# Forget gate of a hybrid decoder block: log-sums formed with heads on partitions instead of tokens

## The chip, the cores and the metric

One core of one Trainium2 chip runs the whole kernel as one program. The metric is device time in microseconds for one execution, median of several runs; lower is better. The core's engines run side by side, each in the order of its own queue: TensorE (PE, matrix products; its weight loads are shown as PEld), VectorE (DVE), ScalarE (ACT), GpSimd (POOL) and SyncE (SP), which here only issues DMA transfers. Products land in PSUM, a memory of eight banks of 128 partitions x 512 f32; everything else is in SBUF, 128 partitions.

## The reference, cut to what matters

One decoder layer on 256 tokens with 1024 channels: RMS norm, one wide input projection, two attention branches of 8 heads each (MoBA and FoX), a gated merge, an output projection and a gated feed-forward with a short convolution, all in float32. The change touches only the forget gate of the FoX branch:

```python
log_f = jax.nn.log_sigmoid(f_logit + b_forget)        # (tokens, 8 heads)
c = jnp.cumsum(log_f, axis=-1)                          # along the 256 tokens, per head
s = q.k * scale + c[t] - c[s]                           # FoX scores: query t, key s
s = where(s_pos <= t_pos, s, -1e30)
p = softmax(s)
```

`f_logit` is the normed input times an 8-column weight. So 8 x 256 numbers are made, summed along the tokens, and used twice: as `c[t]`, one number per query (with tokens on partitions), and as `c[s]`, a row of 256 numbers that every partition needs.

## The kernel before, in words

Tokens are two tiles of 128 (`NT = 2`), channels are eight tiles of 128 (`KT = 8`). Every weight product is made from split operands: a weight half of 128x1024 f32 comes by DMA into `raw`, ScalarE copies its rounded part into `whi` (L131), VectorE subtracts to get the rest, `wlo` (L132), and TensorE makes three products instead of one (L243, L253 for the input projection, L466 to L468 for gate and up projections, and so on). `load` keeps the splitting five halves ahead of use; there are six buffers each for `whi` and `wlo` (`HB = 6`, `AHEAD = 5`) and three for `raw`.

The order on TensorE is that of the program text (`manual_schedule`). All other engines are ordered by a planner that works by priorities, which follow the program text; what stands in `with soon():` gets a priority as if it stood 45 instructions earlier. Each engine then works strictly in the planned order, waiting where an operand is not there.

Around the forget gate the program text runs: `project(3, ...)` (FoX queries), transposes of the MoBA queries, `forget_a`, transposes of the MoBA keys, first half of `project(4)` (FoX keys), `forget_b`, MoBA scores and softmax of head pairs 0 and 1, second half of `project(4)`, `forget_c`, MoBA scores of pairs 2 and 3, `project(5)` (FoX values), `forget_d`, `forget_bias`, then `turn(0)` (transposes of the MoBA probabilities, L432), `gate(0)` and so on; the FoX scores, which read the bias, come after `gate(2)`. `gate(c)` makes 48 products from two weight halves into one bank, and VectorE takes it out into `gates[:, c]` (L475).

The forget gate's own steps:

- `forget_a` makes the logits with heads on partitions: eight products (L318), four at a time in four column groups of 32, so that four partial sums stand on partitions 0-7, 32-39, 64-71 and 96-103 of one bank. Beside them two products (L321) spread `rs`, the norm's factor per token, over all partitions (`rsB`). VectorE copies both out (L323, L324).
- `forget_b` adds up the four partial sums and transposes at once: per token tile, a product with the logits as stationary operand and `sel` (128x8, ones where partition mod 32 is the head) as moving one (L331). The result has tokens on partitions, `z[128, 2, 8]`. Factor and bias are put on by L334, and a chain of small instructions on [128, 16] between ScalarE and VectorE makes the log-sigmoid (L337 to L351).
- `forget_c` sums along the tokens by three products with a triangle of ones and a square of ones (L357 to L359); VectorE copies the result to `cc` (L360), the form with tokens on partitions.
- `forget_d` transposes `cc` back to heads on partitions (L365), copies it out (L367), writes it to a DRAM tile `cd` and reads it back spread over all 128 partitions into `cB`, the upper half of `gates` (L369 and L371, both issued by ScalarE).
- `forget_bias` builds the bias for all 8 heads from `cB`, `cc` and the causal mask: five VectorE instructions on 128x1024 (L378, L380).

`bank()` takes one of the eight PSUM banks. L301 are the transposes of queries and keys, L402 the score products, L414, L417, L419 and L422 the softmax, L611 a product of `ones` with the 256 columns of `sqs` late in the kernel, L595 to L598 GpSimd's sums of squares, L626 and L629 the activation and the product with it in the feed-forward, L479 the sigmoid of the gates.

Of the kernel before, what the change touches and what calls it, by code (L numbers as in the profile page):

```python
# [8 lines left out]
F32 = mybir.dt.float32  # L9
F32R = mybir.dt.float32r  # L10
BF16 = mybir.dt.bfloat16
AF = mybir.ActivationFunctionType
ALU = mybir.AluOpType
# [4 lines left out]
P = 128  # L18
S = 256
NT = 2  # L20
# [3 lines left out]
NH = 8  # L24
# [14 lines left out]
C_G2, C_BG, C_CW, C_CB, C_QG, C_BF, C_GR = 0, 8, 24, 90, 112, 116, 124  # L39
# [4 lines left out]
def decoder_block(ctx, tc, a, out):  # L44
    nc = tc.nc
    sb = ctx.enter_context(tc.tile_pool(name="sb", bufs=1))
    ps = ctx.enter_context(tc.tile_pool(name="ps", bufs=1, space=PSUM))
    dr = ctx.enter_context(tc.tile_pool(name="dr", bufs=1, space=DRAM))
# [3 lines left out]
    def T(shape, tag, bufs=1, dt=F32):  # L52
        return sb.tile(shape, dt, tag=tag, bufs=bufs, name=tag)

    def bank():
        return ps.tile([P, 512], F32, tag="bank", bufs=8, name="bank")
# [91 lines left out]
    gates = T([P, KT, 2, S], "gates")  # L148
    sm = T([P, C_END], "sm")
# [3 lines left out]
    def col(c, n=1):  # L153
        return sm[:, c:c + n]
# [34 lines left out]
    ident = cst[:, 0:128]  # L189
    tri = cst[:, 128:256]  # L190
    ones = cst[:, 256:384]
    mask3 = cst[:, 384:768]
    cos2 = cst[:, 768:832].rearrange("p (t c) -> p t c", t=NT)
    sel = cst[:, 832:840]
# [22 lines left out]
    rs = T([P, NT], "rs")  # L217
# [27 lines left out]
    def project(m, pt, h):  # L245
        for hh in range(2):
            wh, wl = use(("qkv", m - 2, h), hh)
            for k2 in range(2):
                k = 4 * h + 2 * hh + k2
                rh, rl = wh[:, k2 * 512:(k2 + 1) * 512], wl[:, k2 * 512:(k2 + 1) * 512]  # L250
                for i, (lhs, rhs) in enumerate(((xh, rh), (xl, rh), (xh, rl))):
                    for t in range(NT):
                        nc.tensor.matmul(pt[t], lhs[:, k, t * P:(t + 1) * P], rhs, start=(k == 0 and i == 0), stop=(k == KT - 1 and i == 2))  # L253
# [54 lines left out]
    rsB = T([P, S], "rsB")  # L308
    bias = T([P, NH, 384], "bias")
    cc = T([P, NT, NH], "cc")  # L310

    fg = {}

    def forget_a():
# [9 lines left out]
        nc.vector.tensor_copy(rsB, rp)  # L324
        fg["fs"] = fs

    def forget_b():
        fs = fg["fs"]
        ft = bank()
        for t in range(NT):  # L330
            nc.tensor.matmul(ft[:, t * NH:(t + 1) * NH], fs[:, t * P:(t + 1) * P], sel, start=True, stop=True)  # L331
        z = T([P, NT, NH], "z")
        for t in range(NT):
            nc.vector.scalar_tensor_tensor(z[:, t], ft[:, t * NH:(t + 1) * NH], rs[:, t:t + 1], col(C_BF, NH), op0=ALU.mult, op1=ALU.add)  # L334

        az = T([P, NT, NH], "az")
        nc.scalar.activation(az, z, AF.Abs)  # L337
        e = T([P, NT, NH], "ez")
        nc.scalar.activation(e, az, AF.Exp, scale=-1.0)
        u = T([P, NT, NH], "uz")  # L340
        nc.vector.tensor_scalar_add(u, e, 1.0)
        l = T([P, NT, NH], "lz")
        nc.scalar.activation(l, u, AF.Ln)
        d = T([P, NT, NH], "dz")
        nc.vector.scalar_tensor_tensor(d, u, -1.0, e, op0=ALU.add, op1=ALU.subtract)
        r = T([P, NT, NH], "rz")
        nc.vector.reciprocal(r, u)
        nc.vector.tensor_tensor(d, d, r, op=ALU.mult)
        nc.vector.tensor_tensor(l, l, d, op=ALU.subtract)
        lf = T([P, NT, NH], "lf")  # L350
        nc.vector.scalar_tensor_tensor(lf, z, 0.0, l, op0=ALU.min, op1=ALU.subtract)  # L351
        fg["lf"] = lf

    def forget_c():
        lf = fg["lf"]
        cp = bank()
        nc.tensor.matmul(cp[:, 0:8], tri, lf[:, 0], start=True, stop=True)  # L357
        nc.tensor.matmul(cp[:, 8:16], ones, lf[:, 0], start=True, stop=False)
        nc.tensor.matmul(cp[:, 8:16], tri, lf[:, 1], start=False, stop=True)  # L359
        nc.vector.tensor_copy(cc, cp[:, 0:16].rearrange("p (t h) -> p t h", t=NT))  # L360

    def forget_d():
        ctp = bank()
        for t in range(NT):
            nc.tensor.transpose(ctp[:8, t * P:(t + 1) * P], cc[:, t], ident)  # L365
        cT = gates[:NH, 1, 0]
        nc.vector.tensor_copy(cT, ctp[:8, :S])  # L367
        cd = dr.tile([NH, S], F32, name="cd")
        nc.scalar.dma_start(cd, cT)  # L369
        cB = gates[:, 4:].rearrange("p a b t -> p (a b) t")  # L370
        nc.scalar.dma_start(cB, bass.AP(tensor=cd.tensor, offset=cd.offset, ap=[[0, P], [S, NH], [1, S]]))  # L371
        fg["cB"] = cB

    def forget_bias():

# [12 lines left out]
    def scores(br, pairs):  # L388
        if len(pairs) == 2:
            sps = [banks() for _ in pairs]  # L390
            at = [((0, 0), (0, P)), ((1, 0), (1, P))]
        else:
            sps = [banks() for _ in range(3)]
            at = [((0, 0), (0, P)), ((0, 3 * P), (1, 0)), ((2, 0), (1, S)), ((2, P), (2, S))]
        def piece(n, t, j):
            b, o = at[n][t]
            return sps[b][j][:, o:o + (t + 1) * P]
        for t in range(NT):
            ts, us = slice(t * P, (t + 1) * P), slice(0, (t + 1) * P)
            for n, pair in enumerate(pairs):  # L400
                for j, r in enumerate(halves):
                    nc.tensor.matmul(piece(n, t, j), qT[r, pair, ts], kT[r, pair, us], start=True, stop=True)  # L402
        for n, pair in enumerate(pairs):
            softmax(br, pair, [[piece(n, t, j) for t in range(NT)] for j in range(2)])
# [105 lines left out]
    with soon():  # L510
        forget_b()
        scores(0, (0, 1))
    project(4, pk, 1)
    with soon():
        kn, = finish_qk(1, ((1, pk),))
        forget_c()
        scores(0, (2, 3))
    project(5, pv, 0)
    project(5, pv, 1)
    finish_v(pv, 1)  # L520
    with soon():
        forget_d()
        forget_bias()
    turn(0)
    gate(0)
# [148 lines left out]
def _layout(i):  # L674
    f = np.float32
    x = i["x"][0]
    w = i["w_in"][0]
    k128 = lambda m: m.reshape(-1, P, m.shape[1]).transpose(1, 0, 2)
    c = np.ascontiguousarray
    a = {}  # L680
    qkv = w[:, :6 * W4].reshape(2, 4, P, 6, W4)
    a["qkv"] = c(qkv[:, :, :, 2:].transpose(3, 0, 2, 1, 4).reshape(4, 2, P, 2048))
    a["head"] = c(np.concatenate([x.T.reshape(KT, P, S), np.tile(i["attn_norm_g"][0].reshape(KT, P, 1), (1, 1, 8)), qkv[:, :, :, 0:2].reshape(KT, P, 2 * W4)], 2))
    a["wf"] = c(k128(w[:, 6 * W4:6 * W4 + NH]))
    wg = w[:, 6 * W4 + NH:].reshape(KT, P, 2, KT, P)
    a["wg"] = c(wg.transpose(3, 1, 0, 2, 4).reshape(KT, P, 2048))
    wb = np.concatenate([i["w_branch_moba"][0], i["w_branch_fox"][0]]).reshape(KT, P, 4, 256)
    a["wb"] = c(wb.transpose(2, 1, 0, 3).reshape(4, P, 2048))
    wo = i["w_out"][0].reshape(2, 4, P, 2, 2, 256)
    a["wo"] = c(wo.transpose(0, 3, 2, 4, 1, 5).reshape(4, P, 2048))  # L690
    wu = i["w_ffn_up"][0].reshape(KT, P, 2, NF, P)
    a["wu"] = c(wu.transpose(3, 1, 0, 2, 4).reshape(NF, P, 2048))
    a["wd"] = c(i["w_ffn_down"][0].reshape(NF // 2, 2, P, D).transpose(0, 2, 1, 3).reshape(NF // 2, P, 2048))
    sm = np.empty((P, C_END), f)
    a["g1"] = c(i["attn_norm_g"][0].reshape(KT, P).T)
    sm[:, C_G2:C_G2 + 8] = i["ffn_norm_g"][0].reshape(KT, P).T
    sm[:, C_BG:C_BG + 16] = i["b_gate"][0].reshape(2 * KT, P).T
    sm[:, C_CW:C_CW + 66] = i["ffn_conv_w"][0].reshape(3 * NF, P).T
    sm[:, C_CB:C_CB + 22] = i["ffn_conv_b"][0].reshape(NF, P).T
    gm = ["moba_q_norm_g", "moba_k_norm_g", "fox_q_norm_g", "fox_k_norm_g"]  # L700
    for j, n in enumerate(gm):
        sm[0:64, C_QG + j] = sm[64:128, C_QG + j] = i[n][0]
        if j < 2:
            sm[0:16, C_QG + j] = sm[64:80, C_QG + j] = 1.0
            sm[:, C_GR + 16 * j:C_GR + 16 * (j + 1)] = i[n][0][None, 0:16]
    sm[:, C_BF:C_BF + 8] = i["b_forget"][0][None]
    a["smalls"] = sm
    cs = np.zeros((P, 840), f)
    cs[:, 0:128] = np.eye(P)
    tri = np.tril(np.ones((P, P), f))  # L710
    cs[:, 128:256] = tri.T
    cs[:, 256:384] = 1.0
    mask = np.where(tri > 0, f(0), f(BIG))
    cs[:, 384:512] = mask
    cs[:, 640:768] = mask
    inv = np.power(f(500000.0), -np.arange(HALF, dtype=f) * f(2.0) / f(16)).astype(f)
    ang = np.arange(S, dtype=f)[:, None] * inv[None]
    co, si = np.cos(ang), np.sin(ang)
    tab = np.concatenate([co, co, si, -si], 1).reshape(NT, P, 32).transpose(1, 0, 2)
    cs[:, 768:832] = tab.reshape(P, 64)  # L720
    cs[np.arange(P) % 32 < NH, 832 + np.arange(P)[np.arange(P) % 32 < NH] % 32] = 1.0
    a["consts"] = cs
    return a
# [15 lines left out]
```

## Time and profile before

| | |
|---|---|
| median of 3 runs | 365.07 us (364.99 to 365.46) |
| the profiled execution, whole | 365.72 us |
| its span, first to last instruction | 363.9 us |
| granted TensorE clock, mean | 1.000 |
| VectorE waits for ScalarE's `whi` (L132) | 47.6 us, 73 times |
| ScalarE waits for TensorE (L131 behind L467) | 45.9 us, 34 times |

In the profile's page a line such as `L466 PE MATMUL bank<-oh,whi 128*128 128x256 f32 x352 | 97.0, 276 | 0.0` names the source line, the engine, the operation, what is written from what, the shape, the count, the busy time in us, the mean of one in ns, and the idle time of the engine just before. In a timeline a row has start, duration, engine, line and operation, and in brackets how long the engine stood before it and for whom. In the chain of waits a row has the start of a piece, its length on the chain, and what it is; a piece there ends where the next begins, whereas recorded durations of products overlap.

### The profile page before, as it was taken

How to read it: one execution, taken by the hardware profiler on the slowest of the kernel's cores; microseconds unless marked ns; L12 is line 12 of the kernel's file. 1: busy time of each engine (PE TensorE's matmuls, PEld its weight loads, DVE VectorE, ACT ScalarE, POOL GpSimd, SP SyncE). 2: the span in 40 equal slices, each digit the busy share in tenths (PEclk: the TensorE clock that was granted, in tenths of full speed). 3: DMA queues.
4: the chain of work that ended last, by engine and by line, in shares of the span. 5: the costliest groups of instructions: out<-in, count | busy, mean ns of one | idle time of the engine just before them, and what ended most of it. 6: DMA issues, size and time to landing. Idle time of an engine off the chain costs nothing.

```text
span 363.9 us, 7223 instructions
## 1 busy us (share of the span) xinstructions
PE 359.3 (99%) x2975; PEld 340.1 (93%) x2975; DVE 271.9 (75%) x471; ACT 215.0 (59%) x358; POOL 16.2 (4%) x23
## 2 busy tenths in 40 slices
PE   9999999999999999999999999999999999999995
PEld 5888878888999989999999999999999999999995
DVE  4878898971999656984979877768686766768643
ACT  5849566776459885544767645546455546546420
POOL 2520000000000000000530000000000000000000
PEclk9999999999999999999999999999999999999999
DMA  8984666336080653645554654655645554554003
GB/s 276 403 320 189 260 231 212 137 128 222 2 338 21 228 227 122 225 156 200 226 192 156 219 192 170 232 166 183 232 170 183 225 191 166 223 177 173 1 2 115
DMA packets 12001, 68.14 MB, mean 187 GB/s; under 512 B 1592, under 2 KB 2752, under 8 KB 4544
## 3 DMA queue, kind: packets, MB, share of 16 engines
q1 hardware_dynamic: 11664, 66.62, 50.2%
q10 hardware_dynamic: 304, 1.06, 0.9%
q8 instruction: 23, 0.38, 0.4%
q14 instruction: 10, 0.08, 0.1%
HBM read 66.62 MB, written 1.06 MB: 186 GB/s over the span
## 4 chain that ended last, share of the span: by engine, by line
PE 99%; DVE 0%; issue 0%
PE bank L466 15%; PE bank L467 15%; PE bank L468 15%; PE bank L253 12%; PE bank L243 6%; PE bank L652 6%; PE bank L654 5%; PE bank L653 5%; PE bank L556 2%; PE bank L557 2%; PE bank L583 2%; PE bank L558 2%; PE bank L584 2%; PE bank L582 2%; PE bank L402 2%; PE bank L448 2%
## 5 line engine op out<-in xcount | busy, mean ns | idle before, releaser
L132 DVE TENSOR_TENSOR wlo<-raw,whi 128x1024 fp32r<-128x1024 f32 x120 | 146.9, 1228 | 47.8 <-ACT whi L131 47.6
L131 ACT ACTIVATE whi<-raw 128x1024 fp32r<-128x1024 f32 x120 | 126.1, 1058 | 83.0 <-PE bank L467 45.9
L466 PE MATMUL bank<-oh,whi 128*128 128x256 f32 x352 | 97.0, 276 | 0.0
L467 PE MATMUL bank<-ol,whi 128*128 128x256 f32 x352 | 96.8, 275 | 0.0
L468 PE MATMUL bank<-oh,wlo 128*128 128x256 f32 x352 | 96.8, 275 | 0.0
L467 PEld LDWEIGHTS bank<-ol,whi 128*128 128x128 f32 x352 | 66.1, 188 | 0.0
L466 PEld LDWEIGHTS bank<-oh,whi 128*128 128x128 f32 x352 | 66.1, 188 | 0.0
L468 PEld LDWEIGHTS bank<-oh,wlo 128*128 128x128 f32 x352 | 66.1, 188 | 0.0
L466 PE MATMUL bank<-xh,whi 128*128 128x256 f32 x128 | 35.7, 279 | 0.0
L468 PE MATMUL bank<-xh,wlo 128*128 128x256 f32 x128 | 35.3, 276 | 0.0
L467 PE MATMUL bank<-xl,whi 128*128 128x256 f32 x128 | 35.3, 276 | 0.0
L466 PEld LDWEIGHTS bank<-xh,whi 128*128 128x128 f32 x128 | 24.0, 188 | 0.5 <-DVE gates L475 0.3
L467 PEld LDWEIGHTS bank<-xl,whi 128*128 128x128 f32 x128 | 24.0, 188 | 0.0
L468 PEld LDWEIGHTS bank<-xh,wlo 128*128 128x128 f32 x128 | 24.0, 188 | 0.0
L253 PE MATMUL bank<-whi,xh 128*128 128x512 f32 x64 | 20.1, 395 | 0.0
L619 DVE TENSOR_TENSOR sq<-bank,rs 128x512 f32<-128x512 f32 x22 | 15.1, 692 | 6.6 <-PE bank L468 6.5
L253 PE MATMUL bank<-whi,xl 128*128 128x512 f32 x64 | 19.7, 389 | 0.0
L253 PE MATMUL bank<-wlo,xh 128*128 128x512 f32 x64 | 19.7, 388 | 0.0
L556 PE MATMUL bank<-oh,whi 128*128 128x256 f32 x64 | 17.7, 277 | 0.0
L557 PE MATMUL bank<-ol,whi 128*128 128x256 f32 x64 | 17.6, 275 | 0.0
L558 PE MATMUL bank<-oh,wlo 128*128 128x256 f32 x64 | 17.6, 275 | 0.0
L582 PE MATMUL bank<-xh,whi 128*128 128x256 f32 x64 | 17.6, 275 | 0.0
(167 smaller groups left out, 733.0 us busy)
## 6 DMA issues: line engine op xcount, KB each, us to landing
raw<-in_wu SPq DMA_DIRECT2D x22, 1024.0 KB, 4.8
raw<-in_wd SPq DMA_DIRECT2D x11, 1024.0 KB, 4.8
raw<-in_qkv SPq DMA_DIRECT2D x8, 1024.0 KB, 5.0
raw<-in_wg SPq DMA_DIRECT2D x8, 1024.0 KB, 4.8
raw<-in_wb SPq DMA_DIRECT2D x4, 1024.0 KB, 4.8
raw<-in_wo SPq DMA_DIRECT2D x4, 1024.0 KB, 4.8
raw<-in_head SPq DMA_DIRECT2D x6, 512.0 KB, 6.6
gates<-cd ACTq DMA_DIRECT2D x1, 1024.0 KB, 7.4
```

The source lines that it names most:

```text
L131: i = nc.scalar.activation(hi[:, s], raw[:, s], AF.Copy)
L132: d = nc.vector.tensor_tensor(lo[:, s], raw[:, s], hi[:, s].bitcast(F32), op=ALU.subtract)
L243: nc.tensor.matmul(pt[t], lhs[:, k, t * P:(t + 1) * P], rhs, start=(k == 0 and i == 0), stop=(k == KT - 1 and i == 2))
L253: nc.tensor.matmul(pt[t], lhs[:, k, t * P:(t + 1) * P], rhs, start=(k == 0 and i == 0), stop=(k == KT - 1 and i == 2))
L466: nc.tensor.matmul(o, wh[:, w], mh[:, k], start=(k == 0 and i == 0), stop=False)
L467: nc.tensor.matmul(o, wh[:, w], ml[:, k], start=False, stop=False)
L468: nc.tensor.matmul(o, wl[:, w], mh[:, k], start=False, stop=(k == KT - 1 and i == 1))
L556: nc.tensor.matmul(o, wh[:, w], oh[:, 4 * br + k], start=(k == 0), stop=False)
L557: nc.tensor.matmul(o, wh[:, w], ol[:, 4 * br + k], start=False, stop=False)
L558: nc.tensor.matmul(o, wl[:, w], oh[:, 4 * br + k], start=False, stop=(k == 3))
L582: nc.tensor.matmul(o, wh[:, w], mh[:, k], start=(k == 0 and i == 0), stop=False)
L652: nc.tensor.matmul(o, wh[:, w], ah, start=(p == 0 and h == 0 and c == 0), stop=False)
```

## The change

The sums stay with heads on partitions from the start. `forget_b` becomes a single product with `sel` as the stationary operand and all 256 columns of the logits as the moving one, so that 8 partitions x 256 tokens come out, and VectorE multiplies by `rsB`. A new `forget_chain` makes the log-sigmoid on [8, 256]: four ScalarE activations (the reciprocal of `u` is now `exp(-ln u)`), VectorE's addition, difference and minimum, and three steps by GpSimd. Then VectorE sums along the tokens with one scan instruction, and GpSimd issues the two DMAs that spread the result. `forget_c` now makes `cc` from the scan by two transposes of [8, 128] each; it stands where `forget_d` stood, and the old `forget_c`'s place is empty. `forget_chain` stands outside `soon()`, behind the first MoBA scores. The intermediate rows live in parts of `gates` that are not written yet, and the bias per head comes as a column on 8 partitions instead of a row on all.

```diff
+    def row(i):
+        return gates[:NH, i // 2, i % 2]
+
     def forget_b():
-        fs = fg["fs"]
-        ft = bank()
-        for t in range(NT):
-            nc.tensor.matmul(ft[:, t * NH:(t + 1) * NH], fs[:, t * P:(t + 1) * P], sel, start=True, stop=True)
-        z = T([P, NT, NH], "z")
-        for t in range(NT):
-            nc.vector.scalar_tensor_tensor(z[:, t], ft[:, t * NH:(t + 1) * NH], rs[:, t:t + 1], col(C_BF, NH), op0=ALU.mult, op1=ALU.add)
...
-        nc.scalar.activation(az, z, AF.Abs)
...
-        nc.vector.scalar_tensor_tensor(lf, z, 0.0, l, op0=ALU.min, op1=ALU.subtract)
-        fg["lf"] = lf
+        ft = bank()[:NH, 0:S]
+        nc.tensor.matmul(ft, sel, fg["fs"], start=True, stop=True)
+        nc.vector.tensor_tensor(row(1), ft, rsB[:NH], op=ALU.mult)
+
+    def forget_chain():
+        bf = col(C_BF)[:NH]
+        z, az, e, u, l, d, r = (row(i) for i in range(1, 8))
+        nc.scalar.activation(az, z, AF.Abs, bias=bf)
+        nc.scalar.activation(e, az, AF.Exp, scale=-1.0)
+        nc.vector.tensor_scalar_add(u, e, 1.0)
+        nc.scalar.activation(l, u, AF.Ln)
+        nc.scalar.activation(r, l, AF.Exp, scale=-1.0)
+        nc.vector.scalar_tensor_tensor(d, u, -1.0, e, op0=ALU.add, op1=ALU.subtract)
+        nc.gpsimd.tensor_tensor(d, d, r, op=ALU.mult)
+        nc.gpsimd.tensor_tensor(l, l, d, op=ALU.subtract)
+        nc.vector.tensor_scalar(z, z, bf, 0.0, op0=ALU.add, op1=ALU.min)
+        nc.gpsimd.tensor_tensor(z, z, l, op=ALU.subtract)
+        cT = T([NH, S], "cT")
+        nc.vector.tensor_tensor_scan(cT, nc.const_aps.tensor(1.0, (NH, S), F32), z, 0.0, ALU.mult, ALU.add)
+        cd = dr.tile([NH, S], F32, name="cd")
+        nc.gpsimd.dma_start(cd, cT)
+        cB = gates[:, 4:].rearrange("p a b t -> p (a b) t")
+        nc.gpsimd.dma_start(cB, bass.AP(tensor=cd.tensor, offset=cd.offset, ap=[[0, P], [S, NH], [1, S]]))
+        fg.update(cT=cT, cB=cB)
 
     def forget_c():
-        lf = fg["lf"]
-        cp = bank()
-        nc.tensor.matmul(cp[:, 0:8], tri, lf[:, 0], start=True, stop=True)
-        nc.tensor.matmul(cp[:, 8:16], ones, lf[:, 0], start=True, stop=False)
-        nc.tensor.matmul(cp[:, 8:16], tri, lf[:, 1], start=False, stop=True)
-        nc.vector.tensor_copy(cc, cp[:, 0:16].rearrange("p (t h) -> p t h", t=NT))
-
-    def forget_d():
-        ctp = bank()
-        for t in range(NT):
-            nc.tensor.transpose(ctp[:8, t * P:(t + 1) * P], cc[:, t], ident)
-        cT = gates[:NH, 1, 0]
-        nc.vector.tensor_copy(cT, ctp[:8, :S])
-        cd = dr.tile([NH, S], F32, name="cd")
-        nc.scalar.dma_start(cd, cT)
...
-        nc.scalar.dma_start(cB, bass.AP(tensor=cd.tensor, offset=cd.offset, ap=[[0, P], [S, NH], [1, S]]))
-        fg["cB"] = cB
+        cp = bank()[:, 0:16]
+        for t in range(NT):
+            nc.tensor.transpose(cp[:, t * NH:(t + 1) * NH], fg["cT"][:, t * P:(t + 1) * P], ident[:NH, :NH])
+        nc.vector.tensor_copy(cc, cp.rearrange("p (t h) -> p t h", t=NT))
...
     with soon():
         forget_b()
         scores(0, (0, 1))
+    forget_chain()
     project(4, pk, 1)
     with soon():
         kn, = finish_qk(1, ((1, pk),))
-        forget_c()
         scores(0, (2, 3))
...
     with soon():
-        forget_d()
+        forget_c()
         forget_bias()
...
-    sm[:, C_BF:C_BF + 8] = i["b_forget"][0][None]
+    sm[:, C_BF:C_BF + 8] = 0.0
+    sm[0:8, C_BF] = i["b_forget"][0]
```

More of the change, by code (lines that the diff above doesn't have):

```diff
@@ L325, in forget_a @@
         fg["fs"] = fs
+    def row(i):
+        return gates[:NH, i // 2, i % 2]
     def forget_b():
-        fs = fg["fs"]
-        ft = bank()
-        for t in range(NT):
-            nc.tensor.matmul(ft[:, t * NH:(t + 1) * NH], fs[:, t * P:(t + 1) * P], sel, start=True, stop=True)
-        z = T([P, NT, NH], "z")
-        for t in range(NT):
-            nc.vector.scalar_tensor_tensor(z[:, t], ft[:, t * NH:(t + 1) * NH], rs[:, t:t + 1], col(C_BF, NH), op0=ALU.mult, op1=ALU.add)
-        az = T([P, NT, NH], "az")
@@ L337, in forget_b @@
-        nc.scalar.activation(az, z, AF.Abs)
[L338 to L348, printed above, removed]
@@ L349, in forget_b @@
-        nc.vector.tensor_tensor(l, l, d, op=ALU.subtract)
-        lf = T([P, NT, NH], "lf")
-        nc.vector.scalar_tensor_tensor(lf, z, 0.0, l, op0=ALU.min, op1=ALU.subtract)
-        fg["lf"] = lf
-    def forget_c():
-        lf = fg["lf"]
-        cp = bank()
-        nc.tensor.matmul(cp[:, 0:8], tri, lf[:, 0], start=True, stop=True)
-        nc.tensor.matmul(cp[:, 8:16], ones, lf[:, 0], start=True, stop=False)
-        nc.tensor.matmul(cp[:, 8:16], tri, lf[:, 1], start=False, stop=True)
-        nc.vector.tensor_copy(cc, cp[:, 0:16].rearrange("p (t h) -> p t h", t=NT))
@@ L362, in forget_d @@
-    def forget_d():
-        ctp = bank()
-        for t in range(NT):
-            nc.tensor.transpose(ctp[:8, t * P:(t + 1) * P], cc[:, t], ident)
-        cT = gates[:NH, 1, 0]
-        nc.vector.tensor_copy(cT, ctp[:8, :S])
-        cd = dr.tile([NH, S], F32, name="cd")
-        nc.scalar.dma_start(cd, cT)
-        cB = gates[:, 4:].rearrange("p a b t -> p (a b) t")
-        nc.scalar.dma_start(cB, bass.AP(tensor=cd.tensor, offset=cd.offset, ap=[[0, P], [S, NH], [1, S]]))
-        fg["cB"] = cB
+        ft = bank()[:NH, 0:S]
@@ L374, in forget_bias, with forget_c @@
+    def forget_c():
+        cp = bank()[:, 0:16]
+        for t in range(NT):
+            nc.tensor.transpose(cp[:, t * NH:(t + 1) * NH], fg["cT"][:, t * P:(t + 1) * P], ident[:NH, :NH])
+        nc.vector.tensor_copy(cc, cp.rearrange("p (t h) -> p t h", t=NT))
     def forget_bias():
```

## The prediction

> **What bounds the kernel now.** I read the page's first part, then the waits of TensorE alone, then the chain of waits in order of time, and last the timelines of VectorE, ScalarE and GpSimd between 58 and 105 us, where the change lies. First the busy line and the only row that the waits of TensorE hold (engine and line, what it waited for, us in total, times, longest):
>
> ```profile
> PE 359.3 (99%) x2975; PEld 340.1 (93%) x2975; DVE 271.9 (75%) x471; ACT 215.0 (59%) x358; POOL 16.2 (4%) x23
> PE bank L183 <- PEq L732: 0.8, 1, 0.8
> ```
>
> TensorE (PE) is busy for 359.3 of 363.9 us, and its one wait of 0.8 us is at the start of the program. It waits for no other engine afterwards. So only two things can move the end: TensorE's own instructions become fewer or more, or some engine becomes so late that TensorE waits where it does not wait now.
>
> The chain of waits prices TensorE's pieces (start, time on the chain, line, count), since the recorded duration of a pipelined product overlaps its neighbours:
>
> ```profile
> 49.56 0.64 PE bank L301 x16
> 50.20 1.00 PE bank L318 x16
> 58.15 0.34 PE bank L331 x4
> 58.49 1.51 PE bank L402 x16
> 65.66 0.12 PE bank L357 x2
> 65.78 0.22 PE bank L358 x2
> 66.00 0.22 PE bank L359 x2
> 67.73 11.09 PE bank L253 x48
> 78.82 0.22 PE bank L365 x2
> 79.04 1.65 PE bank L432 x48
> 81.01 0.12 PE bank L467
> 104.23 0.31 PE bank L466
> 188.23 0.43 PE bank L611 x2
> ```
>
> The pieces follow each other without a hole (58.15 + 0.34 is L402's 58.49, 67.73 + 11.09 is L365's 78.82). L331, L357 to L359 and L365 are TensorE's whole share of the forget gate behind its eight weight products.
>
> **The change on TensorE.** Removed: L331, 0.34 us; L357 to L359, 0.12 + 0.22 + 0.22 = 0.56 us; L365, 0.22 us; together 1.12 us.
>
> Added: one product with 8 stationary columns and 256 moving columns in f32. Its nearest row is L611, an f32 product of 256 moving columns that also leaves two records: 0.43 us. L318 agrees: eight such products in two rounds (four column groups side by side) take 1.00 us, 0.50 a round. From below, two records as short as L467's 0.12 (256 columns in the other f32 type) would be 0.24; from above, 0.50 is the L318 round. I take 0.43.
>
> Then two transposes that load 8x128 and move 8 columns. L331 also loads 128 columns and moves 8: 0.34 / 4 = 0.085 a record, so 0.17. From below L301's 0.64 / 16 = 0.04 each, 0.08 in all; from above, what the two transposes of L365 take now, 0.22. I take 0.17.
>
> **The sum: -1.12 + 0.43 + 0.17 = -0.52 us**, with ends -1.12 + 0.24 + 0.08 = -0.80 and -1.12 + 0.50 + 0.22 = -0.40. All of it is on the chain.
>
> **The wait that goes.** VectorE (DVE) and ScalarE's queue now show this:
>
> ```profile
> 76.05 2.36 DVE L132 TENSOR_TENSOR wlo<-raw,whi 128x1024 fp32r<-128x1024 f32 x2
> 79.08 0.41 DVE L367 COPY gates<-bank 8x256 f32<-8x256 f32 x1 [0.67 <-PE bank L365]
> 79.52 0.52 ACTq L369 DMA_DIRECT2D cd<-gates  x1
> 82.18 0.35 ACTq L371 DMA_DIRECT2D gates<-cd  x1
> 89.57 2.36 DVE L378 TENSOR_TENSOR bias<-gates,cc 128x1024 f32<-128x1024 f32 x2 [8.85 <-DMA gates<-cd]
> 94.12 1.22 DVE L132 TENSOR_TENSOR wlo<-raw,whi 128x1024 fp32r<-128x1024 f32 x1
> 105.06 0.28 DVE L414 CUSTOM_DVE_ANT_0 s<-bank,bias 128x128 f32<-128x128 f32 x1
> ```
>
> From the first DMA's issue to the bias is 89.57 - 79.52 = 10.05 us, and VectorE stands for 8.85 of it. The change sends both DMAs from GpSimd's queue right behind the scan. Of VectorE's wait little should be left, but I book **nothing** for it: TensorE did not wait. What covers it is stock. The splits show how much (stretch in us, VectorE's busy time in L132 with its count, clock, DMA):
>
> ```profile
> 0.00:94.00 94.00, 37.07 (x32) 1.00 0.63 230
> ```
>
> Ten splits of this line belong to the head weights (two each for k = 0 and 1, one each for the other six) and 16 to the qkv chunks, so 6 of the 32 were gate halves, enough for gates 0 to 2. The next, at 94.12, is first used by gate(3) at 104.23, 8.9 us after its end at 95.34. With that cover, a wait even 8 us longer would cost nothing. Going the other way, the same row says that a wait removed gives nothing: late next is only TensorE's stream itself.
>
> **The chain that takes its place.** Its steps stand on 8 partitions and 256 columns, so they are priced by 256-column rows, and GpSimd's steps by its 256-column sums:
>
> ```profile
> 52.16 0.41 DVE L323 COPY gates<-bank 128x256 f32<-128x256 f32 x1
> L626 ACT ACTIVATE s<-s 128x256 f32<-128x256 f32 x22 | 8.9, 404 | 4.4 <-DVE s L625 4.4
> L479 ACT ACTIVATE gates<-gates,sm 128x256 f32<-128x256 f32 x16 | 7.2, 503 | 2.3 <-DVE gates L475 2.3
> L422 DVE TENSOR_SCALAR s<-s,r 128x256 f32<-128x256 f32 x16 | 5.6, 350 | 0.0
> L629 DVE TENSOR_TENSOR s<-sq,s 128x256 f32<-128x256 f32 x22 | 9.1, 419 | 1.1 <-ACT s L626 1.1
> 174.34 0.86 POOL L595 TENSOR_TENSOR sqs<-sq 128x256 f32<-128x256 f32 x1 [153.26 <-ACT sq L593]
> 178.70 1.67 POOL L598 TENSOR_TENSOR sqs<-sqs,sq 128x256 f32<-128x256 f32 x1
> 180.45 0.81 POOL L597 TENSOR_TENSOR sqs<-sqs,sq 128x256 f32<-128x256 f32 x1
> 178.54 1.23 DVE L132 TENSOR_TENSOR wlo<-raw,whi 128x1024 fp32r<-128x1024 f32 x1
> ```
>
> In series: the multiplication out of PSUM 0.41; Abs with its bias 0.50; Exp 0.40; the addition 0.35; Ln and Exp 0.40 each; three GpSimd steps at 0.86 = 2.58; the scan, which the trace does not show: 0.42 if it streams like L629, 0.84 if each element waits for the one before and it takes twice as long; I take 0.84, the safe end. Sum 5.88 us. `d` and the minimum of `z` lie beside Ln, Exp and GpSimd. TensorE gives the sums free at 58.58 at the latest (58.15 + 0.43), so without queueing the scan ends at 64.5; the transposes are due at 78.82 less the 0.47 us gained ahead of them (0.56 - 0.09), at 78.35. **Slack 13.9 us.** It has to cover queueing, because the chain, unlike the old one, has no raised priority and stands behind two softmax bursts:
>
> ```profile
> 69.18 0.40 ACT L417 ACTIVATE s<-s,nm 128x128 f32<-128x128 f32 x1 [1.73 <-DVE nm L414]
> 72.92 1.99 ACT L131 ACTIVATE whi<-raw 128x1024 fp32r<-128x1024 f32 x2
> 75.14 1.00 DVE L422 TENSOR_SCALAR s<-s,r 128x128 f32<-128x128 f32 x4
> ```
>
> Most orders of the queues fit into it: between the bursts ScalarE even idles 1.73 us before 69.18. The engines' own load hardly changes. ScalarE gets four activations (1.70 us) for three short ones and loses two DMA issues (0.52 + 0.35). On VectorE the multiplication, addition, `d`, minimum and scan (about 2.4 us by the rows above) replace ten short instructions and the 0.41 copy. The softmax results are ready at 76.14 for transposes that begin at 79.04, and the splits have the stock above, so a microsecond on either engine is hidden; if that cover were gone it would cost its own length. GpSimd has been idle for 153.26 us when L595 starts, so nothing is queued behind the chain's steps or its two DMAs there. SP's queue is not touched, the matrix transfers are moved some 10 us earlier, and no other engine waits for them before VectorE's bias.
>
> A DMA issued by GpSimd is not in the trace. Bounds: like ScalarE's, 10.05 us, cB lands between 75 and 82 us; later, it costs nothing until the bias (five instructions, over 6 us) is pushed past its first reader at 105.06 or a split past 104.23, some 15 us later than that. I take zero.
>
> The rows of GpSimd deserve a second look: the same sum takes 0.81 us alone and 1.67 when it starts 0.16 us behind a split of VectorE (178.70 against 178.54). [...]
>
> **The rivals.**
>
> *The chain comes late (slower).* Place: the two transposes on TensorE, before turn(0). If Ln and the second Exp get behind the second softmax burst, they start at 72.92 and end at 73.72; three GpSimd steps at 1.67 end at 78.73; the scan waits up to one split (1.23) and takes 0.84: 80.80. TensorE, due at 78.35, stands 2.45 us: 364.55 + 2.45 = **367.0**. It decides from 78.35 on; at 78.87 the whole gain is eaten, at 79.60 the kernel is measurably slower. For it: no raised priority, full engines, nine changes of engine. Against it: 13.9 us of slack. Chance **0.15**.
>
> *The gain is larger (faster).* The product streams at the lower bound and the transposes too, -0.80: **364.27**. For it: the 8-column load is short. Against it: L611 and L318 agree on 0.43 to 0.50. Chance **0.20**.
>
> *The change saves nothing.* Product and transposes cost what they replace, through switches between shapes that the chain books elsewhere: **365.0**. Against it are the same two rows. Chance **0.07**.
>
> **How the numbers follow.** The profiled execution took 365.72 us, span 363.9 and 1.82 around it; it lies 0.65 above the median of 365.07. The sum makes it 365.20, and the median 365.07 - 0.52 = **364.55 us**. That is 0.14%, and 0.2% (0.73 us) is about what a measurement of this kernel can tell from no change: so the forecast, chance **0.58**, is a gain too small to be seen. Range: down to 364.1 (the bound 364.27 less what three runs scatter), up to 366.0, which takes in no gain, a short stall of 1.45 us, and leaves out some 0.06 below and 0.10 above. Faster 0.20, same 0.58 + 0.07 = 0.65, slower 0.15.
>
> **What would show it.** Right: TensorE's waits still hold only the start; the chain shows about 0.43 for the product, 0.17 for the transposes, nothing at the place of L357 to L359; the VectorE wait for gates<-cd shrinks below 3 us; the scan ends before 78. Wrong: a wait of TensorE on VectorE at the transposes; GpSimd steps of 1.67 in a row; a split that ends after its gate is due; a product of two records that takes 0.24 or 0.8.

## The result, and the profile after

| | before | after |
|---|---|---|
| median, measured side by side | 365.44 us (6 runs, 364.99 to 365.86) | 367.21 us (6 runs, 366.80 to 368.97) |
| ratio after / before | | 1.0061, 95% interval 1.0044 to 1.0079 |
| profiled execution, whole / span | 365.72 / 363.9 us | 368.64 / 366.9 us |

The kernel became slower by 0.6%, 1.8 us. The profiled execution of the changed kernel is one of its two longest; its granted clock is told of below. In the version after, lines behind `forget_bias` stand 12 lower than before: the turn's transposes are L420 (L432 before), `gate(0)` begins with L454 (L466), the splits stay L131 and L132.

The busy line of the page after:

```profile
PE 360.1 (98%) x2967; PEld 339.6 (93%) x2967; DVE 273.5 (75%) x467; ACT 215.2 (59%) x359; POOL 20.4 (6%) x28
```

and the first of the waits of TensorE (engine and line, what it waited for, us in total, times, longest):

```profile
PE bank L420 <- DVE cc L360: 1.6, 1, 1.6
```

TensorE, which waited for no engine before, now waits 1.6 us in the middle of the turn's transposes, for VectorE's copy of `cc`. The view also has two waits of 0.2 us for ScalarE's first splits, at 4.45 and 7.79 us; they lie ahead of all that was changed, and four of the other ten versions' profiles have such waits and six have none, so they are left out of what follows. To see what that costs and what was gained ahead of it, four starts on TensorE are enough: a product near the beginning (L223), the turn's first transpose, the first product of `gate(0)`, the last product. First the timeline of TensorE before (start, duration, what), then after:

```profile
27.18 0.50 PE L223 MATMUL bank<-ones,xss 128*128 128x1 f32 x4
...
78.97 1.72 PE L432 MATMUL bank<-cst,s 64*128 64x64 f32 x48
80.62 0.39 PE L466 MATMUL bank<-xh,whi 128*128 128x256 f32 x1
...
359.78 0.28 PE L654 MATMUL bank<-kT,wlo 128*128 128x256 f32 x1
```

```profile
26.97 0.50 PE L223 MATMUL bank<-ones,xss 128*128 128x1 f32 x4
...
57.87 0.60 PE L332 MATMUL bank<-gates,cst 128*8 128x256 f32 x2
58.40 1.58 PE L390 MATMUL bank<-kT,qT 64*128 64x128 f32 x16
...
78.15 0.28 PE L359 MATMUL bank<-cst,cT 8*128 8x8 f32 x2
78.37 1.28 PE L420 MATMUL bank<-cst,s 64*128 64x64 f32 x33
81.27 0.71 PE L420 MATMUL bank<-cst,s 64*128 64x64 f32 x15 [1.62 <-DVE cc L360]
81.91 0.42 PE L454 MATMUL bank<-xh,whi 128*128 128x256 f32 x1
...
82.55 0.41 PE L454 MATMUL bank<-xh,whi 128*128 128x256 f32 x1
82.77 0.41 PE L455 MATMUL bank<-xl,whi 128*128 128x256 f32 x1
...
85.54 0.28 PE L456 MATMUL bank<-xh,wlo 128*128 128x256 f32 x1
85.66 0.28 PE L454 MATMUL bank<-xh,whi 128*128 128x256 f32 x1
...
362.64 0.28 PE L642 MATMUL bank<-kT,wlo 128*128 128x256 f32 x1
```

- **L223 to the turn:** 78.97 - 27.18 = 51.79 us before, 78.37 - 26.97 = 51.40 after. TensorE's own work shrank by **0.39 us**.
- **The turn:** 80.62 - 78.97 = 1.65 before, 81.91 - 78.37 = 3.54 after, **1.89 more**. The row's bracket says 1.62; the other 0.27 stands in no bracket, and no row shows its cause.
- **From `gate(0)` to the last product:** 279.16 before, 280.73 after, **1.57 more** in this execution. The products of `gate(0)` start every 0.22 us (82.55 to 82.77) where they start every 0.12 us later (85.54 to 85.66). This is the granted clock: in the windows view (stretch, its length, busy time of PE, PEld, DVE, ACT and POOL with counts, then clock, DMA share, GB/s) it shows, from 82 to 86 us,

```profile
66.00:70.00 4.00, 4.00 (x27) 3.15 (x24) 1.77 (x3) 1.56 (x3) 2.83 (x4) 1.00 0.02 4
82.00:84.00 2.00, 2.00 (x10) 2.00 (x11) 2.00 (x3) 1.55 (x4) 0.00 (x0) 0.53 0.98 410
84.00:86.00 2.00, 2.00 (x13) 2.00 (x12) 2.00 (x3) 0.00 (x0) 0.00 (x0) 0.62 0.11 41
```

and 1.00 elsewhere around. The sum, -0.39 + 1.89 + 1.57 = +3.07 us, is what the profiled execution lost. Without the clock it is +1.50, and the four executions after with a mean clock of 0.998 or more took 366.80 to 367.25 us.

Where the copy of `cc` was, the timelines of VectorE, GpSimd and ScalarE tell (in brackets: how long the engine stood before it, and for whom):

```profile
65.20 1.23 DVE L132 TENSOR_TENSOR wlo<-raw,whi 128x1024 fp32r<-128x1024 f32 x1
68.66 0.68 DVE L349 TENSOR_TENSOR_SCAN cT<-const-float32-1.0,gates 8x256 f32<-8x256 f32 x1 [2.23 <-POOL gates L347]
...
76.71 1.23 DVE L132 TENSOR_TENSOR wlo<-raw,whi 128x1024 fp32r<-128x1024 f32 x1
77.85 1.01 DVE L410 TENSOR_SCALAR s<-s,r 128x128 f32<-128x128 f32 x4
78.77 2.36 DVE L132 TENSOR_TENSOR wlo<-raw,whi 128x1024 fp32r<-128x1024 f32 x2
81.04 0.18 DVE L360 COPY cc<-bank 128x16 f32<-128x16 f32 x1
81.25 2.36 DVE L366 TENSOR_TENSOR bias<-gates,cc 128x1024 f32<-128x1024 f32 x2
```

```profile
65.55 1.46 POOL L344 TENSOR_TENSOR gates<-gates 8x256 f32<-8x256 f32 x1 [44.37 <-ACT gates L342]
67.09 0.73 POOL L345 TENSOR_TENSOR gates<-gates 8x256 f32<-8x256 f32 x1
67.90 0.73 POOL L347 TENSOR_TENSOR gates<-gates 8x256 f32<-8x256 f32 x1
...
71.74 0.57 POOL L353 DMA_DIRECT2D gates<-cd  x1 [1.39 <-DMA cd<-cT]
```

```profile
71.89 0.40 ACT L405 ACTIVATE s<-s,nm 128x128 f32<-128x128 f32 x1 [4.33 <-DVE nm L402]
...
75.63 3.89 ACT L131 ACTIVATE whi<-raw 128x1024 fp32r<-128x1024 f32 x4
79.42 1.23 ACT L257 ACTIVATE V<-bank,rs 128x512 f32<-128x512 f32 x2
```

VectorE comes to the scan at 66.4, its order forbids it to go on, and it stands (waits idle) 2.23 us for GpSimd's third step; the window from 66 to 70 has it busy for 1.77 of 4.00 us. Before, that window was full:

```profile
66.00:70.00 4.00, 4.00 (x29) 3.24 (x29) 4.00 (x13) 2.27 (x7) 0.00 (x0) 1.00 0.25 68
```

So everything behind the scan is late by this stand and by the scan's own 0.6 us (68.66 to 69.27), work that VectorE did not have before: the last softmax group starts at 77.85 (75.14 before), the two splits behind it at 78.77 (76.05 before), and the copy of `cc` behind these at 81.04. The copy holds a PSUM bank: two banks are held by the FoX values until ScalarE takes them out, one by `forget_c`'s transposes, and the turn needs six, nine in all for eight. The turn's transposes alternate between the two banks of a pair, 16 a pair, so the 34th is the first in the sixth bank: 33 of the 48 run, and there TensorE stops. ScalarE has the values out by 80.65 (79.42 + 1.23), yet TensorE stands until 81.27: the sixth claim waits for the one bank that the copy gives back, not for any that is free. Before, `forget_d` claimed a bank at the same place, but VectorE stood idle for it (the 0.67 us ahead of the copy at 79.08 in the prediction's rows) and gave it back at once.

This reading (theory A) says: VectorE's stand at the scan makes its queue late, and the bank turns the lateness into a wait of TensorE. Theory B: the late softmax results themselves stop the turn. Theory C: GpSimd's DMA issues hold VectorE up. Theory D: TensorE's gain is lost to something that is not a late queue. A further rival, VectorE's extra work instead of its stand, is named with the experiments that bear on it.

### The profile page after: what moved, and what is told of

It reads as the page before. It is cut to its first block, busy times and chain, and to the rows that moved or that the text cites. A ratio compares the mean times of both kernels' runs of the same rounds, so it can differ in the third digit from the quotient of the medians.

```text
span 366.9 us, 7210 instructions
## 1 busy us (share of the span) xinstructions
PE 360.1 (98%) x2967; PEld 339.6 (93%) x2967; DVE 273.5 (75%) x467; ACT 215.2 (59%) x359; POOL 20.4 (6%) x28
## 4 chain that ended last, share of the span: by engine, by line
PE 91%; DVE 4%; DMA 1%; issue 1%; POOL 1%; ACT 1%; SPq 0%; POOLq 0%; DVEq 0%
PE bank L454 15%; PE bank L456 15%; PE bank L455 15%; PE bank L253 8%; PE bank L642 5%; PE bank L640 5%; PE bank L641 5%; PE bank L243 5%; PE bank L544 2%; PE bank L545 2%; PE bank L571 2%; PE bank L546 2%; PE bank L572 2%; PE bank L570 2%; PE bank L436 2%; DMA gates<-in_head 1%
## 5 line engine op out<-in xcount | busy, mean ns | idle before, releaser
L132 DVE TENSOR_TENSOR wlo<-raw,whi 128x1024 fp32r<-128x1024 f32 x120 | 147.2, 1229 | 54.8 <-ACT whi L131 54.5
L131 ACT ACTIVATE whi<-raw 128x1024 fp32r<-128x1024 f32 x120 | 126.0, 1058 | 86.7 <-PE bank L455 52.6
L454 PE MATMUL bank<-oh,whi 128*128 128x256 f32 x352 | 97.0, 276 | 0.0
L454 PEld LDWEIGHTS bank<-oh,whi 128*128 128x128 f32 x352 | 66.1, 188 | 0.0
L454 PE MATMUL bank<-xh,whi 128*128 128x256 f32 x128 | 36.4, 285 | 0.0
L455 PE MATMUL bank<-xl,whi 128*128 128x256 f32 x128 | 36.1, 282 | 0.0
L454 PEld LDWEIGHTS bank<-xh,whi 128*128 128x128 f32 x128 | 24.7, 193 | 0.5 <-DVE nm L402 0.3
L456 PEld LDWEIGHTS bank<-xh,wlo 128*128 128x128 f32 x128 | 24.8, 194 | 0.0
L455 PEld LDWEIGHTS bank<-xl,whi 128*128 128x128 f32 x128 | 24.8, 194 | 0.0
L405 ACT ACTIVATE s<-s,nm 128x128 f32<-128x128 f32 (+1 forms) x32 | 14.1, 443 | 6.2 <-DVE nm L402 6.2
```

The source lines that it names most:

```text
L131: i = nc.scalar.activation(hi[:, s], raw[:, s], AF.Copy)
L132: d = nc.vector.tensor_tensor(lo[:, s], raw[:, s], hi[:, s].bitcast(F32), op=ALU.subtract)
L454: nc.tensor.matmul(o, wh[:, w], mh[:, k], start=(k == 0 and i == 0), stop=False)
L455: nc.tensor.matmul(o, wh[:, w], ml[:, k], start=False, stop=False)
L456: nc.tensor.matmul(o, wl[:, w], mh[:, k], start=False, stop=(k == KT - 1 and i == 1))
```

## The experiments

Each version is the changed kernel with one edit; two versions put two of these edits together. The table puts TensorE's three stretches against before (51.79, 1.65 and 279.16 us), from the same four starts in each profile; the last column is the median less that of the kernel before on the same chip.

| version | to the turn | in the turn | after it | sum, profiled | median less before |
|---|---|---|---|---|---|
| the change | -0.39 | +1.89 | +1.57 | +3.07 | +1.77 |
| `forget_c` late | -0.61 | +0.35 | +0.19 | -0.07 | +0.05 |
| `cc` by ScalarE | -0.39 | +0.25 | 0.00 | -0.14 | -0.04 |
| one GpSimd step more | -0.39 | +2.35 | -0.01 | +1.95 | +3.53 |
| chain in `soon()` | -0.40 | +1.86 | +1.49 | +2.95 | +3.03 |
| DMAs by ScalarE | -0.39 | +1.08 | -0.02 | +0.67 | +0.62 |
| DMAs by SyncE | -0.39 | +1.89 | +1.61 | +3.11 | +3.02 |
| GpSimd's steps by VectorE | -0.40 | +0.48 | -0.01 | +0.07 | +0.13 |
| the same, `forget_c` late | -0.61 | -0.01 | +0.19 | -0.43 | -0.35 |
| `forget_c` early | -0.19 | 0.00 | -0.01 | -0.20 | -0.11 |
| both: steps by VectorE, early | -0.19 | 0.00 | -0.01 | -0.20 | +0.05 |

Where `forget_c` is late, its transposes (0.2 us) move from the first stretch to the third.

**`forget_c` late** (A against B): the transposes and the copy go behind the turn, so that no bank hangs on VectorE; the stand at the scan stays.

```diff
-    with soon():
-        forget_c()
-        forget_bias()
     turn(0)
     gate(0)
+    with soon():
+        forget_c()
+        forget_bias()
```

> The two transposes of the scan, their copy to cc and the bias go behind turn(0) and gate(0); every engine's order up to 78.8 us stays. Theory A (bank): TensorE stood 1.62 us in turn(0) because its last third needs the PSUM bank that holds those transposes, and that is free only after the copy of cc, which stands behind two splits on a late VectorE. Then no wait of TensorE at L420 above 0.2 us, granted clock 1.00 after 80 us, and 365.4 - 0.5 = about 364.9 us. Theory B (probabilities): TensorE waited for the softmax results of the late VectorE; then a wait of about 1.6 us stays at L420 and the time stays near 367.2. By both, VectorE still stands about 2.2 us for GpSimd ahead of the scan.

365.61 us, ratio 1.0001 (0.9992 to 1.0010). TensorE and VectorE:

```profile
68.80 0.68 DVE L349 TENSOR_TENSOR_SCAN cT<-const-float32-1.0,gates 8x256 f32<-8x256 f32 x1 [2.24 <-POOL gates L347]
77.98 1.01 DVE L410 TENSOR_SCALAR s<-s,r 128x128 f32<-128x128 f32 x4
...
78.27 1.71 PE L420 MATMUL bank<-cst,s 64*128 64x64 f32 x48
80.27 0.39 PE L454 MATMUL bank<-xh,whi 128*128 128x256 f32 x1 [0.29 <-ACT V L257]
```

VectorE stands as long as in the change and its last softmax is as late (77.98 - 27.09 = 50.89 us behind L223's start, 50.88 in the change), yet the 48 transposes run in one go: B falls, the bank is what stopped them. But 364.9 us was missed. The gain went into a second queue made late by the same stand: ScalarE's softmax waits 4.3 us for VectorE, its four splits and the evictions of V come behind it, and `gate(0)` finds no free bank for 0.29 us.

**`cc` by ScalarE** (the same question, the place kept):

```diff
-        nc.vector.tensor_copy(cc, cp.rearrange("p (t h) -> p t h", t=NT))
+        nc.scalar.activation(cc, cp.rearrange("p (t h) -> p t h", t=NT), AF.Copy)
```

> Only the copy of cc moves from VectorE to ScalarE, where it is planned between four splits and the evictions of V, at about 79.5 us. Theory A (bank): the bank is free at about 79.7 instead of 81.2, so TensorE's wait at L420 falls from 1.62 to below 0.3 us, the clock stays at 1.00, about 364.9 to 365.2 us. Theory B (probabilities): VectorE is as late as before, the wait stays at 1.6 us and the time near 367.2.

365.52 us over nine executions, ratio 0.9998 (0.9989 to 1.0007); a tenth execution took 760.18 us at a granted clock of 1.0, and nothing on record shows why. The copy runs at 79.02, no wait is recorded at the turn, and the turn still takes 0.25 us longer than before:

```profile
77.96 1.98 PE L420 MATMUL bank<-cst,s 64*128 64x64 f32 x48
```

The same form took 1.72 us before. I read this as a short stall that shows in no bracket, only in the length of the row; no version tests that reading.

**One GpSimd step more** (a suspected cost enlarged): a copy of [8, 256] ahead of the scan.

```diff
         nc.gpsimd.tensor_tensor(z, z, l, op=ALU.subtract)
+        nc.gpsimd.tensor_copy(row(2), z)
+        z = row(2)
```

> One GpSimd copy on [8, 256] more in the chain, ahead of the scan (0.40 us by the row of such a copy); all else as changed, and VectorE keeps its order. If VectorE's wait at the scan is what makes cc late: that wait 2.23 to about 2.7 us, TensorE's wait at L420 1.62 to about 2.1 us, and the time 0.4 to 0.6 us above the changed kernel's, 367.6 to 367.8. If cc is late only by its place in VectorE's order or by VectorE's own work: nothing changes, 367.2.

369.09 us, ratio 1.0095 (1.0070 to 1.0121).

```profile
69.22 0.68 DVE L351 TENSOR_TENSOR_SCAN cT<-const-float32-1.0,gates 8x256 f32<-8x256 f32 x1 [2.69 <-POOL gates L348]
...
81.81 0.71 PE L422 MATMUL bank<-cst,s 64*128 64x64 f32 x15 [2.08 <-DVE cc L362]
```

VectorE's stand is 2.69 - 2.23 = 0.46 us longer, TensorE's wait 2.08 - 1.62 = 0.46: one for one, nothing in between absorbs any of it. In three of the four executions the granted clock fell as well (means of 0.990, 0.994 and 0.995), so that the median rose by more than the wait and missed the expected time; in the profiled one (367.6 us) it did not (0.998), and the expected time came.

**The chain in `soon()`** (does a higher priority take the stand away?):

```diff
-    forget_chain()
+    with soon():
+        forget_chain()
```

> The chain gets the raised priority that the old one had; nothing else is edited, but the planner then puts its steps ahead of the softmax burst on VectorE and ScalarE. If waiting for GpSimd in a full stretch of VectorE is the cause: VectorE's wait at the scan falls below 0.5 us, VectorE is back to within 0.5 us of its old times at 76 us, TensorE's wait at L420 falls below 0.3 us, and 364.9 to 365.3 us come out. If VectorE's extra work is the cause, it is as late as now and the time stays near 367.

368.59 us, ratio 1.0079 (1.0063 to 1.0094): missed. The scan moved 4.6 us forward, but VectorE's arrival at it moved too:

```profile
64.10 0.68 DVE L349 TENSOR_TENSOR_SCAN cT<-const-float32-1.0,gates 8x256 f32<-8x256 f32 x1 [1.66 <-POOL gates L347]
...
81.43 0.17 DVE L360 COPY cc<-bank 128x16 f32<-128x16 f32 x1
...
81.65 0.78 PE L420 MATMUL bank<-cst,s 64*128 64x64 f32 x15 [1.52 <-DVE cc L360]
```

An earlier stand is nearly as dear as a later one: it is only 0.57 us shorter, VectorE then stands 0.51 us for a split of ScalarE, and counted from L223's start (27.46 in this profile) the copy comes at 53.97 us, in the change at 81.04 - 26.97 = 54.07. The granted clock fell in all four executions (means of 0.993 to 0.995), which is the rest of the time. By its number this is also the outcome named for the rival, VectorE's extra work. Two other versions speak against that rival: one GpSimd step more, which gives VectorE no work, delays the copy by that step, and with GpSimd's steps on VectorE, which gives it three instructions more, the copy comes earlier (below).

**The DMAs by ScalarE** (A against C):

```diff
-        nc.gpsimd.dma_start(cd, cT)
+        nc.scalar.dma_start(cd, cT)
...
-        nc.gpsimd.dma_start(cB, ...)
+        nc.scalar.dma_start(cB, ...)
```

> The changed kernel with cB's two DMAs issued by ScalarE in place of GpSimd, the rest unchanged. Theory A (VectorE stands at the scan for GpSimd's third step, the copy of cc and with it the bank come late): the issues come after the scan, so nothing of the cause is touched; VectorE waits 2.2 us at the scan as before, TensorE 1.6 us at the turn's 34th transpose, 367.2 us. Rival C (GpSimd's queue is busy with DMAs and holds VectorE up behind the scan): TensorE's wait falls below 0.8 us and the time to 366.2 or less.

366.10 us, ratio 1.0017 (1.0008 to 1.0026): C's number.

```profile
68.62 0.68 DVE L349 TENSOR_TENSOR_SCAN cT<-const-float32-1.0,gates 8x256 f32<-8x256 f32 x1 [2.24 <-POOL gates L347]
...
80.18 0.17 DVE L360 COPY cc<-bank 128x16 f32<-128x16 f32 x1
80.26 1.22 DVE L132 TENSOR_TENSOR wlo<-raw,whi 128x1024 fp32r<-128x1024 f32 x1
80.40 0.71 PE L420 MATMUL bank<-cst,s 64*128 64x64 f32 x15 [0.82 <-DVE cc L360]
```

The stand at the scan is unchanged, and so are VectorE's durations. What differs is the planned order: with two issues more on ScalarE the planner put one split, which ran at 76.71 in the change, behind the copy. That can explain the 0.8 us without C, so C needed a version that keeps the order.

**The DMAs by SyncE**: the same edit with `nc.sync`; VectorE's and ScalarE's orders are those of the change, line for line.

> The changed kernel with cB's two DMAs issued by SyncE; the orders of VectorE and ScalarE are word for word those of the changed kernel, which they were not where ScalarE issued them (there one split less stood ahead of the copy of cc). Theory A: the written order of VectorE decides; it waits 2.2 us at the scan, TensorE 1.6 us (1.5 to 1.7) at its 34th transpose, 367.0 us or more. Rival C (GpSimd's DMAs themselves hold VectorE up): TensorE's wait falls to 0.8 us or less, 366.1.

368.66 us, ratio 1.0082 (1.0065 to 1.0098).

```profile
81.33 0.71 PE L420 MATMUL bank<-cst,s 64*128 64x64 f32 x15 [1.63 <-DVE cc L360]
```

No DMA is left on GpSimd, and TensorE's wait is that of the change; the granted clock fell in all four executions (means of 0.994 and 0.995), which is the rest of the time. C falls: GpSimd's issuing is not the cause, and for the 0.8 us the order on VectorE, one split less ahead of the copy, is what remains.

**GpSimd's steps by VectorE** (one part of the change undone):

```diff
-        nc.gpsimd.tensor_tensor(d, d, r, op=ALU.mult)
-        nc.gpsimd.tensor_tensor(l, l, d, op=ALU.subtract)
+        nc.vector.tensor_tensor(d, d, r, op=ALU.mult)
+        nc.vector.tensor_tensor(l, l, d, op=ALU.subtract)
...
-        nc.gpsimd.tensor_tensor(z, z, l, op=ALU.subtract)
+        nc.vector.tensor_tensor(z, z, l, op=ALU.subtract)
```

> The changed kernel with GpSimd's three steps on VectorE, forget_c in its place ahead of turn(0). VectorE's and ScalarE's order up to the copy is that of the version with forget_c behind the turn, where the last softmax ends at 78.5; one split stands ahead of the copy of cc instead of two. Theory A (the bank comes late because VectorE stood for GpSimd): no wait at the scan, the copy at 79.7 to 79.9, TensorE waits 0.2 to 0.3 us at its 34th transpose: 365.5 - 0.4 + 0.3 = 365.4 us. Rival (the place ahead of the turn is bad by itself, whoever does the steps): a wait of over 1 us stays, 366.5 or more.

365.77 us, ratio 1.0005 (0.9996 to 1.0015).

```profile
70.62 0.67 DVE L349 TENSOR_TENSOR_SCAN cT<-const-float32-1.0,gates 8x256 f32<-8x256 f32 x1
...
79.04 1.22 DVE L132 TENSOR_TENSOR wlo<-raw,whi 128x1024 fp32r<-128x1024 f32 x1
80.18 0.17 DVE L360 COPY cc<-bank 128x16 f32<-128x16 f32 x1
...
80.40 0.71 PE L420 MATMUL bank<-cst,s 64*128 64x64 f32 x15 [0.21 <-DVE cc L360]
```

The scan waits for nothing, the copy stands behind one split instead of two, TensorE's wait is 0.21 us as expected. The planner changed VectorE's order here too, but five splits lie between 65 us and the copy in both versions, so the order alone took no split from ahead of it; counted from L223's start the copy comes at 80.18 - 27.52 = 52.66 us, 1.41 earlier than in the change. The time is 0.4 above the 365.4 expected, of which 0.27 is time in the turn outside the bracket, which was not counted (the turn took 2.13, not 1.65 + 0.21); the kernel before, taken as 365.5, had 365.64 on this chip.

**The same with `forget_c` late** (this edit and the first one together; A against D):

> The changed kernel with GpSimd's three steps on VectorE and forget_c with the bias behind turn(0) and gate(0). Theory A: the wait of 2.2 us at the scan goes (what is left is under 0.5, for ScalarE), three steps of 0.4 us come, so the softmax, ScalarE's splits and the evictions of V are about 1 us earlier than with GpSimd; the wait of 0.3 us for V at gate 0 goes, and TensorE's term of -0.39 shows: 365.2 us. Rival D (the 0.39 us is lost to something else than late queues): 365.6, as with GpSimd.

365.13 us against 365.48, ratio 0.9991 (0.9982 to 1.0000). TensorE waits at the start of the program only, the turn takes 1.64 us, and the whole of its gain arrives: no part of it is lost to anything but late queues, and D falls for this version. It is the best version of all, 0.35 us below before, which is less than the 0.2% that a measurement of this kernel can tell from no change.

**`forget_c` early** (the bank given back before the turn), ahead of the last `project(5, pv, 1)`, with GpSimd's steps left in place, and then with them on VectorE:

```diff
     project(5, pv, 0)
+    with soon():
+        forget_c()
     project(5, pv, 1)
     finish_v(pv, 1)
     with soon():
-        forget_c()
         forget_bias()
```

> The changed kernel with forget_c alone moved ahead of the last project(5, pv, 1), so that its transposes stand 5.6 us earlier on TensorE and its bank comes back before the turn. GpSimd's steps stay. Theory A: VectorE still stands 2.2 us at the scan, TensorE waits no more at the turn's transposes. ScalarE's splits and the evictions of V stay late as in the version with forget_c behind the turn (0.3 us at gate 0): 365.56 - 0.39 (TensorE's term as the traces have it) + 0.3 = 365.5 us. Rival B (it is the probabilities that come late): a wait of over 1 us at the turn stays, 367.

> The changed kernel with GpSimd's three steps on VectorE and forget_c ahead of the last project(5, pv, 1). Theory A: no wait of 2.2 us at the scan, no wait of TensorE from the start on, 365.2 us. Rival D: 365.6. If VectorE's order lets the copy of cc come late here too, a wait of TensorE shows at the turn, and the time is above 366.

365.37 us (0.9998, 0.9989 to 1.0007) and 365.53 us (1.0001, 0.9992 to 1.0010). Neither has a wait at the turn, the first with a stand of 2.24 us at the scan still in it: again the bank, and not the stand by itself, carries the cost to TensorE. The 0.3 us at `gate(0)` expected of the first did not come; ScalarE takes the first half of V out from 79.24, and `gate(0)` begins at 80.03.

The second version came to D's number, not to A's 365.2. From L223 on its profile has no wait to lose the time to, and a gain of 0.20 us is there in both profiles; the interval of the medians holds this gain as well as none. It is 0.20 instead of 0.39 because the two transposes cost more here. The first one's timeline:

```profile
71.97 0.61 PE L253 MATMUL bank<-wlo,xh 128*128 128x512 f32 x2
72.52 0.28 PE L359 MATMUL bank<-cst,cT 8*128 8x8 f32 x2
72.73 0.73 PE L253 MATMUL bank<-whi,xh 128*128 128x512 f32 x2
73.30 0.62 PE L253 MATMUL bank<-whi,xl 128*128 128x512 f32 x2
73.76 0.61 PE L253 MATMUL bank<-wlo,xh 128*128 128x512 f32 x2
```

Two weight products take 0.46 us from start to start (73.30 to 73.76), those before and behind the transposes 0.55 and 0.57. By these rows each change between the two kinds of product cost an estimated 0.1 us (0.55 - 0.46 and 0.57 - 0.46), and transposes in a place of their own pay for two changes more than transposes beside the turn's.

## Why the prediction was wrong

- **TensorE's own work**, booked at -0.52 us with ends of -0.80 and -0.40: -0.39. The sign was right; the product takes 58.40 - 57.87 = 0.53 us, not 0.43, and lies just above the upper end of 0.50; the two transposes take 78.37 - 78.15 = 0.22, the upper end, not 0.17. The removed 1.12 us are gone as booked: -1.12 + 0.53 + 0.22 = -0.37. The rival with the larger gain falls.
- **The chain**, 5.88 us in series and the scan's end at 64.5: it took from 58.51 to 69.34 us. The scan's 0.68 us lies between its ends of 0.42 and 0.84 (that it would take twice as long as L629 was the author's estimate, which no row of before shows), GpSimd's 1.46 + 0.73 + 0.73 = 2.92 near the 2.58 booked and far from the 5.01 of the slower rival; the rest is queueing. The 13.9 us of slack up to the two transposes did hold: these waited for nothing, at 78.15.
- **The step that failed** is the sentence behind it: "Most orders of the queues fit into it", and "a microsecond on either engine is hidden". The slack was reckoned for the reader of the scan's result. But the scan is also an instruction in VectorE's queue, and the change adds a wait there, for GpSimd. I did not price that wait, which measured 2.23 us, nor name what stands behind it: the copy of `cc`, for which TensorE then waited 1.62 us. The stretch in which VectorE then stands had no idle time in it before. Its softmax results were ready 2.9 us ahead of their use; the last group starts 2.71 us later after (77.85 against 75.14) and ends at 78.86, behind the turn's first transpose at 78.37. That alone would not have stopped TensorE, as the version with `forget_c` late shows: its readers are only the turn's last 12 transposes.
- **The cover that I named was the wrong one.** I looked at who reads VectorE's results (the softmax, the splits) and not at what its copies give back. The copy of `cc` frees a bank. It stood behind two splits, 2.36 us, that no reader waited for: by their count they are the 30th and 31st, for `gate(1)` and `gate(2)`, and `gate(1)` began only at 93.14.
- **"The engines' own load hardly changes"** was right (VectorE 271.9 to 273.5 us) and of no use: the wait is no load.
- **The bias and its DMAs** went as forecast: VectorE's wait of 8.9 us for `gates<-cd` is gone, the transfer was issued at 71.74 and took 6.5 us, and cB landed at 78.2, between the 75 and 82 of the bounds. It was worth nothing, as booked, since TensorE had not waited.
- **The slower rival** named 367.0 us, and 367.21 came, but not by its mechanism: its place was the two transposes, its condition GpSimd's steps behind the second softmax burst. The steps ran ahead of that burst, and TensorE stopped 33 transposes later. That the times agree is chance.
- **Of the signs**, the scan's end before 78, VectorE's wait under 3 us and the empty place of L357 to L359 showed "right". That TensorE's waits hold only the start showed "wrong", and at a place where the prediction did not look: the turn's transposes, not those that read the scan.

Of GpSimd's three steps, the one of 1.46 us started at 65.55, 0.35 us behind a split of VectorE (65.20 to 66.43); the two of 0.73 us ran while VectorE stood. In the version with the chain in `soon()`, the first step took 0.74 us with no split beside it. By these rows the split beside it lengthened VectorE's stand by an estimated 0.7 us (1.46 - 0.73); why it does so, no run shows. The prediction's 0.81 us on GpSimd was not "alone": VectorE's L591 ran beside it (179.68, 1.85 us for two), so a busy VectorE by itself did not lengthen that sum.

## What to carry to other kernels

A hand-over to another engine and back cost here the wait of the engine that takes the result back, in its own queue (VectorE's 2.23 us at the scan): slack of the final reader says nothing about what is queued behind that wait. Count banks as well as operands: a small copy that frees a PSUM bank is on the path of whoever claims that bank next (here a copy of 0.18 us, for which TensorE waited 1.62), and should stand ahead of work that is only stock. A planner that knows durations may change the order of three instructions elsewhere for an edit as small as a DMA's engine, so compare the orders before an edit is credited with a change of time.

## What the runs showed of the hardware

**Behind a stop of 1.5 to 1.6 us the granted clock was halved for 3.4 us in three profiles.** In the change, products start every 0.21 to 0.22 us up to 85.54 and every 0.12 us from there on; the lower clock sets in at about 82.1 (the window from 82.0 to 82.5 has 0.61), and the granted clock is 0.50 from 82.5 to 85.5. The windows from 82 to 84 and from 84 to 86 us have 0.53 and 0.62 in the change, 0.54 and 0.61 with the chain in `soon()`, and 0.60 and 0.55 with the DMAs by SyncE; with the GpSimd step more, whose stop was longer (2.08 us), both have 1.00. Of the versions whose TensorE waited 1.5 us or more in the turn, 13 of 18 executions had a mean clock of 0.990 to 0.995 (2 of 6 of the change, 4 of 4 in `soon()`, 3 of 4 with the GpSimd step more, 4 of 4 with the DMAs by SyncE), and 5 one of 0.998 or 0.999. None of the 74 executions of the other seven versions, with waits of 0 to 0.82 us, had one below 0.997. In the three profiles the drop costs 1.5 to 1.6 us (+1.57, +1.49 and +1.61 in the table's third stretch), as much as the wait. Why the same wait is followed by the drop in some executions and not in others, no run here shows.

**In the turn, a wait's bracket understated what it cost.** In the six versions in which the turn has one (0.21, 0.82, 1.52, 1.62, 1.63, 2.08 us), the turn grew by the bracket and 0.26 to 0.34 us more.
